# Experts of a two-block network in rounds of 1024 inner features, on one Trainium2 core

## The chip, the core and the metric

The program runs on one core of one Trainium2 chip. The core has five engines with a queue each, which run side by side and wait for each other by semaphores: TensorE (PE; its weight loads are shown apart as PEld), VectorE (DVE), ScalarE (ACT), GpSimd (POOL) and SyncE (SP), which here issues nearly all DMAs. Matrix products land in PSUM, which has eight banks of 128 partitions x 512 float32. The metric is the device time of one execution in microseconds (us). The kernel before takes 2576.64 us, the median of three runs (2575.73 to 2576.72).

## What is computed

Two blocks of a network run one after the other on 256 tokens of 1024 features, all in float32. The first block has two layers of attention; the second of them is followed by a mixture of experts, and this is the part that the change touches:

```python
def swiglu(h, wg, wu, wd):
    return (jax.nn.silu(h @ wg) * (h @ wu)) @ wd

def moe_swiglu(h, router, wg, wu, wd):
    logits = (h @ router).astype(jnp.float32)
    top_vals, top_idx = lax.top_k(logits, TOP_K)          # 2 of 8 experts for each token
    gates = jax.nn.softmax(top_vals, axis=-1)
    gate_e = jnp.sum(jax.nn.one_hot(top_idx, N_EXPERTS) * gates[..., None], axis=-2)
    ...
    for e in range(N_EXPERTS):
        out = out + gate_e[..., e:e + 1] * swiglu(h, wg[e], wu[e], wd[e])
    return out
```

`wg[e]` and `wu[e]` are 1024 x 3584, `wd[e]` is 3584 x 1024: 44.04 MB for one expert, 352 MB for eight. The second block (a gated feed-forward on tokens and on 256 context tokens, a mixer of a long convolution and attention, a second feed-forward) needs, among other things, the context's feed-forward, which depends on nothing of the first block; its pieces are strewn into the first block's stages as filling work.

## The kernel before

**Products.** A float32 operand is split into two parts, `hi` (rounded) and `lo` (the rest), whose sum is exact; `split` (L128 to L131) does it with a copy on ACT (L130) and a subtraction on DVE (L131). `mm3` (L133 to L137) makes one product of three: hi x hi (L135), hi x lo (L136), lo x hi (L137), each a matmul with 512 columns into one PSUM bank. So a weight must pass DMA, then ACT, then DVE, before L136 can use it.

**Weights.** They come in parts of 1 MB: a tile `raw` of 128 partitions x 2048 numbers, four buffers, loaded by one DMA on SP's queue (`wload`, L85). `wsplit` (L90) splits a part in two halves of 1024 numbers each into the tiles `whi` and `wlo`, three buffers each. `cuts` (L117) says what a part holds: for n columns of the matrix, 2048/n blocks of 128 rows. With n = 512 a part is four row blocks, and each row piece in memory is 512 numbers (2 KB); with n = 1024 it is two row blocks with pieces of 4 KB. Each part feeds 12 matmuls where 128 tokens are worked on, 24 where it is 256.

**The experts** (`moe`, L768 to L847). An expert takes at most 128 tokens. `gather` collects them by products with a 0/1 matrix (`xgh`, `xgl`: 32 small matmuls through the banks `mm`). Then, for f0 = 0, 512, ... 3072 (seven rounds), `ffn_gate` multiplies by 512 columns of `wg` (two parts, 24 matmuls, one PSUM bank `lin0`), ACT takes the silu of it (L313), `ffn_turn` transposes the round before's products (`hd` to `hh`, `hl`), `ffn_up` multiplies by 512 columns of `wu` (two parts, 24 matmuls), DVE multiplies silu and up (`hd`, L325), and `ffn_down` multiplies the round before's `hh`, `hl` by four row blocks of `wd` (two parts, 24 matmuls) into the two banks `acc`, which collect over all seven rounds. At the end of an expert `result` splits the sums into the tiles `yh`, `yl`, and `scatter` brings them back to their tokens (eight matmuls through banks `mm`), during the second round of the next expert. `hook("chunk")` puts in a piece of the context's work at every third round.

**PSUM.** Three banks `mm`, four `acc`, one `tp` (L71 to L82), the same for the whole program.

**Order.** The framework under the kernel plays the program through with costs of its own and writes the order of each engine's queue from that: a matmul that would have to wait can be put behind a later one, and splits stand ahead of what uses them as far as their buffers and the expected arrival of the data let them. On the chip each queue then runs strictly in that order. So where ACT's queue has a silu that waits for PE, the splits behind it wait, too; the same holds for `hd` on DVE.

## Time and profile before

The profile is of one execution, 2576.6 us from its first to its last instruction, which is also its device time to within 0.1 us. The stage of the experts is the stretch from about 703 to 1785 us.

| | share of the span |
|---|---|
| PE busy | 97% (2511.3 us, 12201 matmuls) |
| PEld busy | 78% |
| DVE busy | 71% (77 to 88% in the experts' stage) |
| ACT busy | 57% (70 to 76% in the experts' stage) |
| DMA | 71% of 16 engines (87 to 99% in the experts' stage) |

How to read it: a matmul with 512 columns is shown with 0.39 us from its start to its end, but the next one starts 0.23 us after it, so that PE's busy time covers up small waits; they show in the distance between starts, and in the weight loads (PEld), which stand idle in front of a matmul whose weights or data are late. The DMA share is that of the 16 DMA engines' time spent on packets.

### The profile page before, as it was taken

To read this page: it belongs to the slowest core of one execution; us is meant where nothing else is said; L and a number is where in the kernel's file an instruction comes from. 1 tells how busy PE (TensorE), PEld (TensorE's weight loads), DVE (VectorE), ACT (ScalarE), POOL (GpSimd) and SP (SyncE) were. 2 spreads that over 40 slices of the span, in tenths; PEclk is the share of its full clock that TensorE was granted. 3 is DMA by queue.
4 is the path that set the end of the run, shared out by engine and by line. 5 is a ranking of instruction groups with operands and counts; after the bars stand their busy time and mean duration, and the time that the engine had idled before them with its cause. 6 is when DMAs were issued, how large, how long until landed. Compare 5 with 4: busy or idle time off the path is not lost.

```text
span 2576.6 us, 31558 instructions
## 1 busy us (share of the span) xinstructions
PE 2511.3 (97%) x12201; PEld 2014.7 (78%) x12201; DVE 1818.5 (71%) x2272; ACT 1471.9 (57%) x1963; POOL 107.1 (4%) x128
## 2 busy tenths in 40 slices
PE   8999999999899999999999999999999999899998
PEld 5777777777788888888778787887778888777887
DVE  4655544656678888888888888888655667866444
ACT  3554333455477777777777777777443556434433
POOL 1000000110000000000000000000000110200000
PEclk9999999999999999999999999999999999999999
DMA  7746777544489999999999999997755553355552
GB/s 275 246 153 238 272 246 261 167 154 157 127 309 324 334 338 329 345 339 344 339 343 360 342 364 351 353 341 271 250 180 183 205 169 95 107 189 180 187 180 82
DMA packets 302175, 646.05 MB, mean 251 GB/s; under 512 B 16275, under 2 KB 43716, under 8 KB 301636
## 3 DMA queue, kind: packets, MB, share of 16 engines
q1 hardware_dynamic: 296164, 638.74, 71.3%
q10 hardware_dynamic: 5856, 5.24, 0.6%
q8 instruction: 97, 1.59, 0.2%
q14 instruction: 58, 0.48, 0.1%
HBM read 637.56 MB, written 6.38 MB: 250 GB/s over the span
## 4 chain that ended last, share of the span: by engine, by line
PE 62%; DVE 5%; ACT 2%; DMA 2%; issue 1%; POOL 1%; POOLq 0%; DVEq 0%; ACTq 0%
PE lin L136 13%; PE lin L137 13%; PE lin L135 13%; PE acc L136 5%; PE acc L135 5%; PE acc L137 5%; DVE wlo L131 2%; PE tp L180 2%; ACT whi L130 1%; PE gather L785 1%; DMA raw<-in_moe_w_up 1%; DMA raw<-in_moe_w_gate 1%; DVE dmx L1353 1%; PE z L136 0%; PE z L135 0%
## 5 line engine op out<-in xcount | busy, mean ns | idle before, releaser
L131 DVE TENSOR_TENSOR wlo<-raw,whi 128x1024 fp32r<-128x1024 f32 x1108 | 1312.2, 1226 | 414.8 <-ACT whi L130 411.9
L130 ACT ACTIVATE whi<-raw 128x1024 fp32r<-128x1024 f32 x1108 | 1115.7, 1055 | 613.2 <-PE lin L137 271.2
L135 PE MATMUL lin<-whi,hTh 128*128 128x512 f32 (+1 forms) x1152 | 449.1, 391 | 3.3 <-ACT hTh L130 2.8
L136 PE MATMUL lin<-wlo,hTh 128*128 128x512 f32 (+1 forms) x1152 | 444.8, 387 | 0.5 <-DVE wlo L131 0.5
L137 PE MATMUL lin<-whi,hTl 128*128 128x512 f32 (+1 forms) x1152 | 444.7, 386 | 0.6 <-DVE hTl L131 0.6
L136 PE MATMUL lin<-wlo,xgh 128*128 128x512 f32 x896 | 356.0, 397 | 4.8 <-DVE wlo L131 4.4
L135 PE MATMUL lin<-whi,xgh 128*128 128x512 f32 x896 | 354.3, 395 | 0.0
L137 PE MATMUL lin<-whi,xgl 128*128 128x512 f32 x896 | 350.7, 391 | 0.0
L136 PE MATMUL acc<-wlo,hh 128*128 128x512 f32 x736 | 290.3, 394 | 0.8 <-DVE wlo L131 0.7
L137 PE MATMUL acc<-whi,hl 128*128 128x512 f32 x736 | 288.4, 392 | 0.4 <-DVE hl L131 0.4
L135 PE MATMUL acc<-whi,hh 128*128 128x512 f32 x736 | 282.8, 396 | 2.3 <-ACT hh L130 2.3
L135 PEld LDWEIGHTS lin<-whi,hTh 128*128 128x128 f32 x1152 | 218.5, 190 | 52.7 <-ACT hTh L130 3.8
L136 PEld LDWEIGHTS lin<-wlo,hTh 128*128 128x128 f32 x1152 | 218.5, 190 | 47.1 <-DVE wlo L131 4.0
L137 PEld LDWEIGHTS lin<-whi,hTl 128*128 128x128 f32 x1152 | 218.1, 189 | 47.4 <-DVE hTl L131 1.7
L136 PEld LDWEIGHTS lin<-wlo,xgh 128*128 128x128 f32 x896 | 168.8, 188 | 51.3 <-DVE wlo L131 17.6
L135 PEld LDWEIGHTS lin<-whi,xgh 128*128 128x128 f32 x896 | 168.8, 188 | 35.9 <-issue 0.4
L137 PEld LDWEIGHTS lin<-whi,xgl 128*128 128x128 f32 x896 | 168.8, 188 | 33.8
L135 PEld LDWEIGHTS acc<-whi,hh 128*128 128x128 f32 x736 | 138.1, 188 | 35.1 <-ACT hh L130 3.4
L136 PEld LDWEIGHTS acc<-wlo,hh 128*128 128x128 f32 x736 | 138.3, 188 | 32.7 <-DVE wlo L131 2.8
L137 PEld LDWEIGHTS acc<-whi,hl 128*128 128x128 f32 x736 | 138.1, 188 | 30.5 <-DVE hl L131 0.8
L313 ACT ACTIVATE sg<-lin 128x512 f32<-128x512 f32 (+1 forms) x94 | 54.9, 584 | 116.4 <-PE lin L137 116.3
L131 DVE TENSOR_TENSOR hl<-tp,hh 128x512 fp32r<-128x512 f32 (+1 forms) x106 | 71.4, 674 | 68.5 <-ACT hh L130 68.0
(390 smaller groups left out, 2438.8 us busy)
## 6 DMA issues: line engine op xcount, KB each, us to landing
raw<-in_moe_w_gate SPq DMA_DIRECT2D x112, 1024.0 KB, 6.5
raw<-in_moe_w_up SPq DMA_DIRECT2D x112, 1024.0 KB, 6.6
raw<-in_moe_w_down SPq DMA_DIRECT2D x112, 1024.0 KB, 6.7
raw<-in_w_ff_in SPq DMA_DIRECT2D x66, 1024.0 KB, 5.4
raw<-in_w_in SPq DMA_DIRECT2D x58, 1024.0 KB, 5.4
raw<-in_w_ada SPq DMA_DIRECT2D x36, 1024.0 KB, 7.0
raw<-in_w_ff_out SPq DMA_DIRECT2D x33, 1024.0 KB, 5.0
raw<-in_dense_w_gate SPq DMA_DIRECT2D x14, 1024.0 KB, 8.1
```

Source lines behind the costliest of these rows:

```text
L130: self.nc.scalar.activation(hi, src, AF.Copy)
L131: self.nc.vector.tensor_tensor(lo, src, hi.bitcast(F32), op=ALU.subtract)
L135: t.matmul(out, ah, bh, start=first, stop=False)
L136: t.matmul(out, ah, bl, start=False, stop=False)
L137: t.matmul(out, al, bh, start=False, stop=last)
L180: nc.tensor.transpose(tp[:, b * P:(b + 1) * P], src[:, (b0 + b) * P:(b0 + b + 1) * P], self.ident)
L313: self.nc.scalar.activation(s, p, AF.Silu)
L785: nc.tensor.matmul(p[:, b * CAP:(b + 1) * CAP], src[:, t, k * P:(k + 1) * P], Dm[:, t, e], start=t == 0, stop=t == NT - 1)
L1353: nc.vector.tensor_reduce(mx[:, m:m + 1], ps, axis=AX.X, op=ALU.max)
```

## The change

Experts work in rounds of 1024 inner features: f0 = 0, 1024, 2048 with 1024 columns and f0 = 3072 with 512, four rounds in place of seven. The gate and up weights of a wide round come as parts of two row blocks x 1024 columns (row pieces of 4 KB), four parts each; the last round has parts as before. Each part feeds two PSUM banks, `lin0` (the first 512 columns) and `lin1`. The transposes of the round before come in two batches, after gate and in the middle of up. The `down` step of a wide round has four parts. `result` no longer has tiles of its own: it takes the tiles `hh`, `hl` (one buffer each). In the experts' stage PSUM is shared out as five banks `mm`, two `xacc`, one `tp`; what asks for `acc` there gets an `mm`. Scatter moves to the middle of the second round's gate. The filling pieces of the context come at every 1.7th round instead of every third. (In the changed file the comments are gone, and line numbers are 10 to 50 higher.)

```diff
+    def banks(self, **n):
+        self.psst.close()
+        self.nbank = n
+        self.ps = self.psst.enter_context(self.tc.tile_pool(name="ps", bufs=1, space=PSUM, reuse_waits="tile"))
+
+    def bank(self, tag, name):
+        tag = tag if tag in self.nbank else "mm"
+        return self.ps.tile([P, 512], F32, tag=tag, bufs=self.nbank[tag], name=name)
...
-            first = [(ap, m, 512) for f0 in (0, 512) for w in (wg, wu) for _, m, ap in self.cuts(w[0], 0, KT, f0, 512)]
+            first = [(ap, m, 1024) for w in (wg, wu) for _, m, ap in self.cuts(w[0], 0, KT, 0, 1024)]
             self.run_ahead(first[:7], 2)
             self.overflow(hk, og, cnt_i)
+            self.banks(mm=5, xacc=2, tp=1)
...
                 def result(job):
-                    yh = pool.tile([P, D], F32R, tag="yh", bufs=1, name="yh")
-                    yl = pool.tile([P, D], F32R, tag="yl", bufs=1, name="yl")
+                    yh, yl = (v.rearrange("p b s -> p (b s)") for v in self.expert_h(pool))
...
+                rounds = [(f0, min(1024, F1 - f0)) for f0 in range(0, F1, 1024)]
...
-                    for f0 in range(0, F1, 512):
-                        job = dict(f0=f0, n=512, nt=1, hT=xg, e=e)
-                        self.ffn_gate(pool, job, wg[e])
+                    for f0, n in rounds:
+                        job = dict(f0=f0, n=n, hT=xg, e=e)
+                        pg = self.expert_lin(xg, wg[e], f0, n, lambda: e and f0 == 1024 and scatter(e - 1, y))
+                        s = [self.ffn_silu(pool, p) for p in pg]
                         if prev:
-                            self.ffn_turn(pool, prev)
-                        self.ffn_up(pool, job, wu[e])
-                        if f0 + 512 == F1 and e + 1 < NE:
-                            nxt = gather(e + 1)
+                            self.expert_turn(pool, prev, 0)
+                        pu = self.expert_lin(xg, wu[e], f0, n, lambda: prev and self.expert_turn(pool, prev, 1))
+                        job["hd"] = [self.ffn_gated(pool, *v) for v in zip(s, pu)]
+                        if f0 + n == F1 and e + 1 < NE:
+                            xg = gather(e + 1)
                         if prev:
                             if prev["f0"] == 0:
-                                acc = [[self.acc(f"acc0{h}") for h in range(2)]]
+                                acc = [self.bank("xacc", f"acc0{h}") for h in range(2)]
...
-                            self.ffn_down(prev, wd[prev["e"]], F1)
+                            self.expert_down(prev, wd[prev["e"]])
...
+    def expert_lin(self, xT, w, c0, n, half=None):
+        out = [self.mm(f"lin{h}")[:, :min(512, n - 512 * h)] for h in range(-(-n // 512))]
+        for k0, m, (wh, wl) in self.parts(w, 0, KT, c0, n):
+            if half and k0 == KT // 2:
+                half()
+            for h, o in enumerate(out):
+                hs = slice(h * 512, h * 512 + o.shape[1])
+                for k in range(k0, k0 + m):
+                    self.mm3(o, xT[0][:, k], xT[1][:, k], wh[:, k - k0, hs], wl[:, k - k0, hs], k == 0, k == KT - 1)
+        return out
+
+    def expert_h(self, pool):
+        return [pool.tile([P, 8, CAP], F32R, tag=v, bufs=1, name=v) for v in ("hh", "hl")]
...
-                  "chunk": every(3, lambda: both(1), 2),
+                  "chunk": every(1.7, lambda: both(1), 1),
                   "last": lambda: both(40)})
+        self.banks(mm=3, acc=4, tp=1)
```

How this moves instructions shows best at the end of `up`, where DVE's `hd` (silu times up) stands between splits of weights. This is DVE's queue before, in the sixth expert's second round; `wlo_11197` and `wlo_11205` are the parts of `up`, `wlo_11239` is the first part of `down`, and "x2" is both halves of a part:

```order
L131 TENSOR_TENSOR wlo_11197<-raw_11194,whi_11196 128x1024 x2
L131 TENSOR_TENSOR wlo_11205<-raw_11202,whi_11204 128x1024 x2
L131 TENSOR_TENSOR wlo_11239<-raw_11236,whi_11238 128x1024
L325 SCALAR_TENSOR_TENSOR hd_11234<-sg_11182,lin0_11193 128x512
L131 TENSOR_TENSOR wlo_11239<-raw_11236,whi_11238 128x1024
L131 TENSOR_TENSOR wlo_11247<-raw_11244,whi_11246 128x1024 x2
```

And now, in the fifth expert's third round; `wlo_11372` is the last part of `up`, `wlo_11396` the first of `down`:

```order
L142 TENSOR_TENSOR wlo_11345<-raw_11342,whi_11344 128x1024 x2
L142 TENSOR_TENSOR wlo_11372<-raw_11369,whi_11371 128x1024 x2
L336 SCALAR_TENSOR_TENSOR hd_11389<-sg_11287,lin0_11300 128x512
L336 SCALAR_TENSOR_TENSOR hd_11391<-sg_11289,lin1_11301 128x512
L142 TENSOR_TENSOR wlo_11396<-raw_11393,whi_11395 128x1024 x2
L142 TENSOR_TENSOR wlo_11416<-raw_11413,whi_11415 128x1024 x2
```

Before, a half of the first `down` part is split ahead of `hd`; now two `hd` stand ahead of both halves. PE's queue at the same place before; `whi_11238` and `wlo_11239` are the first `down` part, and `tp` is the transpose of this round's `hd`:

```order
L137 MATMUL lin0_11193<-whi_11204,xgl_10586 128x512
L135 MATMUL acc00_10933<-whi_11238,hh_11184 128x512
L135 MATMUL acc01_10934<-whi_11238,hh_11184 128x512
L136 MATMUL acc00_10933<-wlo_11239,hh_11184 128x512
L137 MATMUL acc00_10933<-whi_11238,hl_11185 128x512
L136 MATMUL acc01_10934<-wlo_11239,hh_11184 128x512
L137 MATMUL acc01_10934<-whi_11238,hl_11185 128x512
L135 MATMUL acc00_10933<-whi_11238,hh_11184 128x512
L135 MATMUL acc01_10934<-whi_11238,hh_11184 128x512
L180 MATMUL tp_11321<-ident_69,hd_11234 128x128 x4
L136 MATMUL acc00_10933<-wlo_11239,hh_11184 128x512
```

And now, from the last products of `up` on:

```order
L146 MATMUL lin1_11301<-whi_11371,xgh_10525 128x512
L147 MATMUL lin0_11300<-wlo_11372,xgh_10525 128x512
L148 MATMUL lin0_11300<-whi_11371,xgl_10526 128x512
L147 MATMUL lin1_11301<-wlo_11372,xgh_10525 128x512
L148 MATMUL lin1_11301<-whi_11371,xgl_10526 128x512
L146 MATMUL acc00_11108<-whi_11395,hh_11291 128x512
L146 MATMUL acc01_11109<-whi_11395,hh_11291 128x512
L191 MATMUL tp_11533<-ident_69,hd_11389 128x128 x4
L147 MATMUL acc00_11108<-wlo_11396,hh_11291 128x512
```

Before, eight products and the transposes stood between the end of `up` and the first product with the second half of `wlo`; now the first product with `wlo` comes after two products and the transposes. At the end of the last expert, where nothing but `result` stands between the last product and `scatter`, PE's queue was, before (`yh`, `yl` are result's tiles):

```order
L806 MATMUL scatter_14943<-yh_14937,DT_5424 128x512
L806 MATMUL scatter_14947<-yh_14937,DT_5424 128x512
L806 MATMUL scatter_14951<-yh_14937,DT_5424 128x512
L807 MATMUL scatter_14943<-yl_14938,DT_5424 128x512
L807 MATMUL scatter_14951<-yl_14938,DT_5424 128x512
L807 MATMUL scatter_14947<-yl_14938,DT_5424 128x512
L806 MATMUL scatter_14955<-yh_14937,DT_5424 128x512
```

And now, with five banks `mm`:

```order
L817 MATMUL scatter_14899<-hh_14893,DT_5424 128x512
L817 MATMUL scatter_14903<-hh_14893,DT_5424 128x512
L817 MATMUL scatter_14907<-hh_14893,DT_5424 128x512
L817 MATMUL scatter_14911<-hh_14893,DT_5424 128x512
L818 MATMUL scatter_14899<-hl_14894,DT_5424 128x512
```

The fourth product into a bank of its own no longer comes last.

## Rows read from the trace of the kernel before

**Rows 1.** The page's head.
```profile
span 2576.6 us, 31558 instructions
```

**Rows 2.** Windows of the stage: us, busy time of each engine (instructions), clock, DMA share, GB/s.
```profile
974.00:1110.00 136.00, 136.00 (x655) 113.54 (x654) 119.68 (x118) 97.56 (x109) 0.00 (x0) 1.00 0.96 340
1371.00:1498.00 127.00, 125.68 (x580) 102.27 (x579) 111.88 (x109) 94.84 (x109) 0.00 (x0) 1.00 0.99 352
1498.00:1629.00 131.00, 131.00 (x606) 107.10 (x606) 115.36 (x112) 98.85 (x113) 0.00 (x0) 1.00 0.98 355
```

**Rows 3.** Timeline of PE: start, us, instruction; experts 5 to 8 begin, last scatter.
```profile
1240.45 0.34 PE L785 MATMUL gather<-Dm,h_hi 128*128 128x128 f32 x2
...
1370.45 0.45 PE L785 MATMUL gather<-Dm,h_hi 128*128 128x128 f32 x3
...
1497.75 0.45 PE L785 MATMUL gather<-Dm,h_hi 128*128 128x128 f32 x3
...
1623.44 0.45 PE L785 MATMUL gather<-Dm,h_hi 128*128 128x128 f32 x3
...
1784.35 0.40 PE L807 MATMUL scatter<-yl,DT 128*128 128x512 f32 x1
```

**Rows 4.** Timeline of PE in a stretch without waits, `lin` of the third expert.
```profile
989.65 0.39 PE L135 MATMUL lin<-whi,xgh 128*128 128x512 f32 x1
...
994.42 0.39 PE L135 MATMUL acc<-whi,hh 128*128 128x512 f32 x1
```

**Rows 5.** The chain of waits, merged: start, us, what.
```profile
945.48 0.44 PE tp L180 x4
...
974.20 3.52 PE gather L785 x32
```

**Rows 6.** Waits from 1243 to 1785 us: total us, times, longest.
```profile
ACT whi L130 <- DMA raw<-in_moe_w_gate: 17.9, 20, 2.5
ACT whi L130 <- DMA raw<-in_moe_w_down: 15.5, 19, 3.3
PEld lin L136 <- DVE wlo L131: 14.8, 28, 1.2
...
PEld acc L136 <- DVE wlo L131: 2.8, 5, 1.0
```

**Rows 7.** DMA queue from 1393 to 1402 us: packets, MB, share of 16 engines.
```profile
q1 hardware_dynamic: 1647, 3.28, 100.6%
```

**Rows 8.** The same from 1387 to 1391 us, and from 1460 to 1465.
```profile
q1 hardware_dynamic: 401, 1.55, 97.7%
...
q1 hardware_dynamic: 501, 1.86, 102.9%
```

**Rows 9.** Timeline of DVE around an `hd`, fifth expert.
```profile
1319.76 3.50 DVE L131 TENSOR_TENSOR wlo<-raw,whi 128x1024 fp32r<-128x1024 f32 x3 [1.07 <-ACT whi L130]
1323.88 0.69 DVE L325 SCALAR_TENSOR_TENSOR hd<-sg,lin 128x512 f32<-128x512 f32 x1 [0.63 <-PE lin L137]
1324.49 5.76 DVE L131 TENSOR_TENSOR wlo<-raw,whi 128x1024 fp32r<-128x1024 f32 x5
```

**Rows 10.** Timeline of PE at the same place.
```profile
1323.46 0.39 PE L137 MATMUL lin<-whi,xgl 128*128 128x512 f32 x1
...
1325.51 0.60 PE L180 MATMUL tp<-ident,hd 128*128 128x128 f32 x4
1325.86 0.48 PE L136 MATMUL acc<-wlo,hh 128*128 128x512 f32 x1
```

**Rows 11.** Timeline of ACT: `result` of the last expert.
```profile
1780.20 0.60 ACT L130 ACTIVATE yh<-acc 128x512 fp32r<-128x512 f32 x1
1781.56 0.60 ACT L130 ACTIVATE yh<-acc 128x512 fp32r<-128x512 f32 x1 [0.76 <-PE acc L137]
```

**Rows 12.** Timeline of PE: the last product and a late scatter.
```profile
1781.13 0.39 PE L137 MATMUL acc<-whi,hl 128*128 128x512 f32 x1
...
1784.01 0.51 PE L806 MATMUL scatter<-yh,DT 128*128 128x512 f32 x1 [0.37 <-DVE x L808]
```

More of the change, by code (lines that the diff above doesn't have):

```diff
@@ L77, in tp @@
         if wide and self.turn:
[L78 to L79 removed]
+            return self.bank("acc", "tpa")
+        return self.bank("tp", "tp")
     def acc(self, name="acc"):
[L82 removed]
+        return self.bank("acc", name)
     def wload(self, ap, kt, n):
@@ L791, in result @@
                 def result(job):
-                    yh = pool.tile([P, D], F32R, tag="yh", bufs=1, name="yh")
-                    yl = pool.tile([P, D], F32R, tag="yl", bufs=1, name="yl")
+                    yh, yl = (v.rearrange("p b s -> p (b s)") for v in self.expert_h(pool))
                     for h in range(2):
                         hs = slice(h * 512, (h + 1) * 512)
-                        self.split(yh[:CAP, hs], yl[:CAP, hs], job["acc"][0][h][:CAP])
+                        self.split(yh[:CAP, hs], yl[:CAP, hs], job["acc"][h][:CAP])
                     return yh, yl
@@ L832, in moe @@
                                     nc.scalar.activation(DT[:CAP, e0:e0 + 2].rearrange("p e s -> p (e s)"), tp[:CAP], AF.Copy)
-                            self.ffn_down(prev, wd[prev["e"]], F1)
+                            self.expert_down(prev, wd[prev["e"]])
                             if f0 == 0:
                                 y = result(prev)
-                        if f0 == 512 and e > 0:
-                            scatter(e - 1, y)
                         if not self.ahead:
@@ L840, in moe @@
                         prev = job
-                    xg = nxt
                 hook("last")
@@ L844, in moe, with expert_turn, expert_down @@
                 prev["acc"] = acc
-                self.ffn_turn(pool, prev)
-                self.ffn_down(prev, wd[NE - 1], F1)
+                for i in range(2):
+                    self.expert_turn(pool, prev, i)
+                self.expert_down(prev, wd[NE - 1])
                 scatter(NE - 1, result(prev))
+    def expert_lin(self, xT, w, c0, n, half=None):
[10 more added lines that the diff above has]
+        return [pool.tile([P, 8, CAP], F32R, tag=v, bufs=1, name=v) for v in ("hh", "hl")]
+    def expert_turn(self, pool, job, i):
+        if i == 0:
+            job["h"] = self.expert_h(pool)
+        if 512 * i < job["n"]:
+            bs = slice(4 * i, 4 * i + job["hd"][i].shape[1] // P)
+            self.transposes(job["hd"][i], bs.stop - bs.start, hl=[v[:, bs] for v in job["h"]])
+    def expert_down(self, job, wd):
+        hh, hl = job["h"]
+        b0, nb = job["f0"] // P, job["n"] // P
+        for k0, m, (wh, wl) in self.parts(wd, b0, nb, 0, D):
+            order = [(k, h) for k in range(m) for h in range(2)]
+            if k0 + m == F1 // P:
+                order.sort(key=lambda v: v[1])
+            for k, h in order:
+                hs = slice(h * 512, (h + 1) * 512)
+                self.mm3(job["acc"][h], hh[:, k0 + k - b0], hl[:, k0 + k - b0], wh[:, k, hs], wl[:, k, hs],
+                         k0 + k == 0, k0 + k == F1 // P - 1)
     def overflow(self, hk, og, cnt_i):
@@ L1564, in run @@
         self.moe({"norm": lambda: ctx(1), "logits": lambda: ctx(1), "pos": lambda: ctx(1), "cnt": lambda: ctx(1),
-                  "chunk": every(3, lambda: both(1), 2),
+                  "chunk": every(1.7, lambda: both(1), 1),
                   "last": lambda: both(40)})
+        self.banks(mm=3, acc=4, tp=1)
         self.dbg("x_f1", self.x)
```

12 lines of the change are left out of this document (4 added, 8 removed).

## The prediction

> **What bounds the kernel now.** I read the windows of the stage first, to see which engine is full. In the sixth and seventh expert (the last two windows) PE is busy all the time or nearly, at the full granted clock (1.00, which is 2.4 GHz), and the DMA engines are at a share of 0.98 to 0.99 with 352 to 355 GB/s; DVE has 12% to spare, ACT a quarter [rows 2]. So two things are full at once, and the question is which of them gives way to the other. A busy PE hides small waits, so I then read starts in PE's timeline: where nothing waits, 21 products take 994.42 - 989.65 = 4.77 us, 0.227 us each [rows 4]. A batch of four transposes costs 0.44 us, a gather 3.5 us [rows 5]. From the program's order an expert has 336 products for gate and up, 168 for down and 8 for scatter: 512 x 0.227 = 116.3, seven batches 3.1, gather 3.5, together 122.9 us. The starts of the gathers [rows 3] give what it took: 130.0 us for the fifth expert, 127.3 for the sixth, 125.7 for the seventh. The sixth and seventh have two more batches each from the context, 123.8 us of work. The eighth, up to its last scatter, took 160.9 us, with 639 products and ten batches, 153.0 us of work. So PE lost 7.1 + 3.5 + 1.9 + 7.9 = 20.4 us in these four, and that is what there is to win here. The first four experts have the context's products between them, which use each weight twice; in the third the DMA share is 0.96 and PE busy throughout [rows 2]. I count nothing to be won there.
>
> The list of waits says what PE lost it to: its weight loads stood 14.8 us for the `wlo` of gate and up and 2.8 us for that of down, and behind that ACT waited 17.9 us for gate weights and 15.5 us for down weights [rows 6]. So in the second half of the stage the data come late, by a little.
>
> The profiled execution's span is 2576.6 us [rows 1], the median of the timed runs 2576.64; I add the sum to the former and need no correction.
>
> **The change part by part.** What it does not touch: the number of products, of transposes, of splits on ACT and DVE, of bytes and of 1 MB DMAs on SP's queue, and the counts of filling pieces (18 calls in either case, in like places). None of these gets a price.
>
> *Wide rows.* In three rounds of four the gate and up weights come in pieces of 4 KB in place of 2 KB. The trace has both kinds. A stretch with gate and up alone moved 3.28 MB in 9 us at a share of 1.006, which is 362 GB/s for full engines [rows 7]. Two stretches with down, whose rows are 4 KB today, give 397 and 362 GB/s [rows 8]. So the wide pieces are worth between nothing and 9.5%; I take the mean, 4.7%. It acts on 6/7 of two thirds of the bytes, 57%: 2.7% of the transfer time, which is about 125 us for an expert (127 us at 0.98). That is 3.4 us for an expert, but no more than it lost: 3.4 + 3.4 + 1.9 + 3.4 = 12.1 us, and as buffers are few some half microsecond stays in each: -10 us. The bounds are 0 (the lower end of the rate) and -17.6 (all that the weight loads stood for).
>
> The Trainium skill, "Perfetto Trace Analysis", section "DMA Optimizations", says that making transfers of 2 KB into 4 KB can improve the throughput dramatically where it binds. These rows show a few per cent at most; by the rule the term would be its far bound, -17.6, and the sum some 7 us lower.
>
> *DVE's queue at the end of up.* This is the term against. Before, DVE has at least one half of the first down part split when it comes to `hd`. In the changed queue this cover is gone in the last four experts: going through their twelve wide rounds, I count four in which both `hd` stand ahead of any `wlo` of down, and four in which one half stands between the two `hd`. In the first four experts one part or more stands ahead nearly everywhere. What it costs follows from a place today where the cover is just enough: `hd` starts 0.42 us after the start of the last product of up (1323.46 to 1323.88), DVE goes on 0.61 us later (1324.49), a half of `wlo` takes 5.76 / 5 = 1.15 us [rows 9], and PE takes it up some 0.1 us after that: at 1325.86 [rows 10], without losing anything, because eight products and the transposes stood between. Put the end of up at 0. In the new order `lin0` is complete two products before, its `hd` runs from about -0.25 to 0.35, the second to 0.95, a half of `wlo` ends at 2.1 and PE can go on at 2.2; it has two products and four transposes to do, 0.9 us. So it loses 1.3 us in each of the four rounds of the first kind. In the other kind the first half ends at 1.5, PE goes on at 1.6 and has lost 0.7; it then has six products, 1.36 us, and the second half, behind the second `hd`, can be used at 3.35: another 0.4. Sum: 4 x 1.3 + 4 x 1.1 = 9.6 us. The bounds are 0, where DVE's queue is behind anyway because data are late (the wait is then the same one), and 8 x 2.0 = 16, where no transposes fill. I take 9.6, as DVE stood idle 0.63 us before `hd` even with the half ahead of it [rows 9].
>
> *Result without tiles of its own.* `yh` could be written while PE was in its last six products; the copy of the first half began 1.4 us before that of the second [rows 11]. `hh` has one buffer, so now both copies come after the last product that reads it, 1781.13 + 0.43 at the end [rows 12]. The second copy is then late by half a microsecond, and ACT's and DVE's later splits with it. Eight ends of experts, half of them with one part ahead: +2 us, with bounds of 0 and 8 x 0.5 = 4. Against that, scatter has five banks: the wait for an earlier result's addition goes (0.37 us, [rows 12]), and the four products with `hh` can come first: -0.5 us at the end of the last expert, where nothing else covers it. In the other experts scatter lies between gate's parts, hidden either way.
>
> *Silu and transposes.* Two silus after 48 products cost ACT what two after 24 each did; before the second, ACT has one part of up ready in most rounds, as before. The second batch of transposes in the middle of up is the same 0.44 us. The new banks let `lin1`'s products go ahead while `wlo` is late, which makes gate and up more patient by two products. I price this at 0 and give it ±3.
>
> *The switch of banks.* It comes once on each side of the stage. On the near side PE stands for the branch around the overflow code anyway; on the far side the norm's transposes get banks that the last filling products may still hold. 0, within ±2.
>
> Sum: -10 + 9.6 + 2 - 0.5 = +1.1 us: 2576.6 + 1.1 = 2577.7 us.
>
> **The rivals.**
>
> *The data win (faster).* DVE's queue costs nothing because the same waits are there already, only elsewhere: late data hold PE at gate, DVE's pause lets the buffers fill, and what counts is the transfer time alone. For it: ACT waits for DMA nearly twice as long as PE is held (33.4 against 17.6 us, [rows 6]), and the DMA share is at its top. Against it: PE and not DMA was the fuller one in the seventh expert, which lost just 1.9 us. Then -10 is left with result's +2 and -0.5 and a part of DVE's price, 1: -7.5, 2569 us; at the far bound of the rate, 2561.
>
> *DVE's queue decides (slower).* Its place is the pair of `hd` at the end of up; its price the full 1.3 to 2.0 us in eight rounds, and some in the first four experts, 14 us; result costs 3. It decides from the point at which the wide rows bring less than 12 us. With the lower rate they bring 5: +12, 2589 us. For it: the cover was 0.5 part in most of these rounds, and rows 10 show that this was just enough. Against it: a pause of PE lets DMA run ahead, so part of the price is given back.
>
> *Wide rows bring nothing.* The limit is not in the packets but in the memory behind them: then the two stretches of 362 GB/s [rows 7, 8] are the rule and 397 the exception. Late data stay, DVE's pauses fall partly into them: 0 + 6 + 1.5, 2584 us.
>
> The Trainium skill, "DMA: Bandwidth & Descriptors", section "Where 436 GB/s comes from", speaks for this last one: it puts the limit of transfers out of HBM at about 358 GB/s for a core, which the 352 to 355 GB/s of the windows would have reached. The 397 GB/s of rows 8 speak against it.
>
> **How the numbers follow.** My forecast, no change to within its parts, 0.40; the data win 0.30; DVE's queue decides 0.18; wide rows bring nothing 0.12. A measurement of this kernel can tell some 0.2% from no change, 5.2 us: below 2571.4 is faster, above 2581.8 slower. The first rival is faster, the two others are slower, the forecast's own spread (2572 to 2582) is the same: faster 0.30, same 0.40, slower 0.30. The likeliest time is 2577.7. The range runs from 2564 to 2590: on either side it takes in a rival's time and leaves out its far end. The forecast's own range is 2572 to 2582.
>
> **What would show it.** Right: the four last experts together within 3 us of today's 543.9 us (1240.45 to 1784.35); PE's waits for the `wlo` of gate and up down by half, new ones for that of down, of about a microsecond, each behind a pair of `hd`; the DMA share there lower by 0.02 to 0.03. Wrong towards faster: no `wlo` waits at down longer than 0.5 us, and experts of 124 us. Wrong towards slower: these waits in the first four experts, too, or a DMA share of 0.98 still. The forecast also fails if the stage is as forecast and the norm after it starts later, which would be the banks or `result`.

## The result, and the profile after

The changed kernel takes 2589.47 us (median of 4 runs, 2587.57 to 2593.02), the kernel before 2576.18 us in its 4: ratio 1.0056, 95% interval 1.0044 to 1.0068. It is slower by some 13 us. The forecast of no change, 2577.7 us, was wrong; the time lies just inside the upper edge of its range, 2590 us.

The profiled execution of the changed kernel is the slowest of its four; it is 14.6 us longer than the one of before:

```profile
span 2591.2 us, 31548 instructions
```

Where the 14.6 us are, from the starts of gathers and of the last scatter. PE's timeline after has for the first, the fifth to the eighth gather and the last scatters (each row starts with us from the span's start):

```profile
704.20 1.09 PE L797 MATMUL gather<-Dm,h_hi 128*128 128x128 f32 x4 [7.41 <-PEq L903]
...
1246.45 1.45 PE L797 MATMUL gather<-Dm,h_hi 128*128 128x128 f32 x12
...
1373.25 0.33 PE L797 MATMUL gather<-Dm,h_hi 128*128 128x128 f32 x2
...
1501.54 0.33 PE L797 MATMUL gather<-Dm,h_hi 128*128 128x128 f32 x2
...
1628.95 0.33 PE L797 MATMUL gather<-Dm,h_hi 128*128 128x128 f32 x2
...
1793.68 1.10 PE L818 MATMUL scatter<-hl,DT 128*128 128x512 f32 x4
```

| us | before | after | difference |
|---|---|---|---|
| start to first gather | 703.4 | 704.2 | +0.8 |
| experts 1 to 4 | 537.1 | 542.3 | +5.2 |
| experts 5 to 8, to the start of the last scatter matmul (1784.35 [rows 3]; 1794.37 after) | 543.9 | 547.9 | +4.0 |
| from there to the end | 792.3 | 796.8 | +4.6 |

PE has as many products in these stretches as before (4311 of 512 columns in the eight experts, split between the halves to within one). So not even a third of the loss lies in the last four experts, where the forecast had its two large terms. The waits of experts 5 to 8 (1249 to 1795 us; total us, times, longest), beside [rows 6]:

```profile
ACT whi L141 <- DMA raw<-in_moe_w_gate: 24.1, 18, 3.9
...
ACT whi L141 <- DMA raw<-in_moe_w_down: 17.5, 22, 2.0
...
PEld lin L147 <- DVE wlo L142: 11.9, 25, 1.0
...
PEld acc L147 <- DVE wlo L142: 9.1, 10, 1.3
```

For gate and up the weight loads wait 2.9 us less than before, for down 6.3 us more. The transfer itself did what the forecast said. The windows of experts 6 and 7 (busy time of each engine, clock, DMA share, GB/s):

```profile
1373.00:1501.00 128.00, 126.28 (x580) 102.27 (x579) 111.96 (x110) 94.22 (x109) 0.00 (x0) 1.00 0.95 348
1501.00:1629.00 128.00, 126.85 (x585) 103.13 (x584) 112.39 (x109) 95.16 (x110) 0.00 (x0) 1.00 0.96 350
```

The share fell by 0.02 to 0.04 against [rows 2]; 348/0.95 is 366 GB/s for full engines where 352/0.99 was 356, 350/0.96 is 365 where 355/0.98 was 362: a rate higher by some 3% and under 1%. But ACT waits longer for the data of gate and of down than before.

Three kinds of places show the loss. *First, the end of up* (the place of [rows 9, 10], in the fifth expert; DVE's timeline, then PE's):

```profile
1285.95 1.28 DVE L336 SCALAR_TENSOR_TENSOR hd<-sg,lin 128x512 f32<-128x512 f32 x2
1287.15 3.49 DVE L142 TENSOR_TENSOR wlo<-raw,whi 128x1024 fp32r<-128x1024 f32 x3
```
```profile
1285.51 0.61 PE L146 MATMUL acc<-whi,hh 128*128 128x512 f32 x2
1286.69 0.66 PE L191 MATMUL tp<-ident,hd 128*128 128x128 f32 x4 [0.56 <-DVE hd L336]
1288.43 0.50 PE L147 MATMUL acc<-wlo,hh 128*128 128x512 f32 x1 [1.08 <-DVE wlo L142]
```

Both `hd` stand ahead of the first half of down, and PE stands 1.08 us for it (1.24 us by the distance of starts, which is used below). This is the forecast's mechanism at its forecast price of 1.3 us; four places of the last four experts have it.

*Second, a filling piece in the third expert.* DVE, PE, and the granted clock (the column behind POOL's busy time) there:

```profile
1091.25 1.29 DVE L1160 TENSOR_TENSOR ctx_y<-cacc,ctx_y 128x512 f32<-128x512 f32 x2 [1.71 <-PE cacc L148]
1092.45 1.22 DVE L142 TENSOR_TENSOR wlo<-raw,whi 128x1024 fp32r<-128x1024 f32 x1
1093.59 1.28 DVE L1160 TENSOR_TENSOR ctx_y<-cacc,ctx_y 128x512 f32<-128x512 f32 x2
1094.79 5.76 DVE L142 TENSOR_TENSOR wlo<-raw,whi 128x1024 fp32r<-128x1024 f32 x5
```
```profile
1094.21 0.48 PE L146 MATMUL lin<-whi,xgh 128*128 128x512 f32 x1
1097.19 0.69 PE L147 MATMUL lin<-wlo,xgh 128*128 128x512 f32 x1 [2.51 <-DVE wlo L142]
1097.68 0.63 PE L148 MATMUL lin<-whi,xgl 128*128 128x512 f32 x1
```
```profile
1093.00:1097.20 4.20, 1.69 (x11) 1.15 (x9) 4.20 (x6) 2.49 (x3) 0.00 (x0) 1.00 0.32 119
1097.20:1100.60 3.40, 3.40 (x8) 2.69 (x9) 3.40 (x4) 0.00 (x0) 0.00 (x0) 0.52 0.94 326
```

DVE's queue has the additions for the context, which wait for PE's last products of the piece, ahead of the splits that PE needs next. PE stands 2.5 us (2.8 us by the distance of starts); then its granted clock is 0.52, the level of 1.2 GHz, and eight products start 0.43 us apart instead of 0.23: 1.6 us more. These 4.4 us are most of what experts 1 to 4 lost; the kernel before has no wait of over 0.5 us there.

*Third, the norm behind the stage.* PE's timeline, before and after:

```profile
1794.02 1.09 PE L287 MATMUL tpa<-ident,xg 128*128 128x128 f32 x8 [1.37 <-DVE xg L277]
```
```profile
1801.90 0.49 PE L147 MATMUL lin<-wlo,hTh 128*128 128x512 f32 x1 [1.29 <-DVE wlo L142]
1804.94 1.97 PE L298 MATMUL tpa<-ident,xg 128*128 128x128 f32 x8 [2.54 <-DVE xg L288]
...
1807.56 0.63 PE L147 MATMUL lin<-wlo,hTh 128*128 128x512 f32 x1
1807.99 0.63 PE L148 MATMUL lin<-whi,hTl 128*128 128x512 f32 x1
```

From the last scatter matmul to the norm's first transposes 26 filling products stand in PE's order; before it was 32 (the expectations below count one more each). With fewer of them PE stands 2.54 us before the transposes (1.37 before), and the lower clock follows again (starts 0.43 us apart at the end of the rows). By PE's starts, 4.2 of the 4.6 us behind the stage are lost by the end of this norm.

### The profile page after: what moved, and what is told of

The parts are those of the page before. It is cut to its first block, busy times and chain, and to the rows that moved or that the text cites. A ratio compares the mean times of both kernels' runs of the same rounds, so it can differ in the third digit from the quotient of the medians.

```text
span 2591.2 us, 31548 instructions
## 1 busy us (share of the span) xinstructions
PE 2518.2 (97%) x12201; PEld 2017.5 (78%) x12201; DVE 1818.4 (70%) x2272; ACT 1471.4 (57%) x1963; POOL 109.0 (4%) x128
## 4 chain that ended last, share of the span: by engine, by line
PE 64%; DVE 4%; ACT 2%; issue 1%; DMA 1%; POOL 1%; ACTq 0%; POOLq 0%; DVEq 0%
PE lin L147 13%; PE lin L148 13%; PE lin L146 13%; PE acc L147 5%; PE acc L148 5%; PE acc L146 5%; DVE wlo L142 2%; PE tp L191 2%; PE gather L797 1%; ACT whi L141 1%; DMA raw<-in_moe_w_gate 1%; DVE dmx L1399 1%; PE z L147 1%; PE z L146 0%; PE z L148 0%
## 5 line engine op out<-in xcount | busy, mean ns | idle before, releaser
L146 PE MATMUL lin<-whi,xgh 128*128 128x512 f32 x896 | 343.7, 396 | 0.0
L141 ACT ACTIVATE hh<-tp 128x512 fp32r<-128x512 f32 (+1 forms) x106 | 61.9, 584 | 95.6 <-PE tp L191 83.1
```

Source lines behind the costliest of these rows:

```text
L141: self.nc.scalar.activation(hi, src, AF.Copy)
L146: t.matmul(out, ah, bh, start=first, stop=False)
```

## The experiments

Ratios are to the kernel before, with 95% intervals; "stage" is first gather to last scatter and "behind" from there to the end, both of the profiled execution; "clock" is the mean over the timed runs. A profile is a single execution: the fastest of its kernel's in h21, e5_chunk0 and gcov, the slowest in the changed kernel, nbcov, nbcovg0 and pool4. So differences of a microsecond or two in these columns say little.

| run | edit | median us (runs) | ratio, interval | stage | behind | clock |
|---|---|---|---|---|---|---|
| before | | 2575.84 (27) | | 1081.0 | 792.3 | 0.9926 |
| after | | 2589.47 (4) | 1.0056, 1.0044 to 1.0068 | 1090.2 | 796.8 | 0.9913 |
| e1_narrow | 2 KB pieces | 2593.25 (5) | 1.0064, 1.0050 to 1.0078 | 1092.4 | 795.5 | 0.9904 |
| e3_cover | down split ahead of `hd` | 2589.13 (5) | 1.0050, 1.0037 to 1.0064 | 1085.5 | 795.6 | 0.9914 |
| h21 | `hh` in halves | 2588.43 (5) | 1.0054, 1.0041 to 1.0068 | 1087.6 | 794.2 | 0.9914 |
| e5_chunk0 | pieces one round earlier | 2587.09 (5) | 1.0047, 1.0033 to 1.0061 | 1082.1 | 793.9 | 0.9908 |
| tail | switch before the scatter | 2589.57 (5) | 1.0053, 1.0040 to 1.0066 | 1090.0 | 792.3 | 0.9922 |
| b_banks | before, with the banks alone | 2578.88 (11) | 1.0013, 1.0004 to 1.0021 | 1079.3 | 795.6 | 0.9915 |
| c0cov | pieces and cover | 2582.89 (7) | 1.0030, 1.0019 to 1.0041 | 1081.1 | 796.7 | 0.9910 |
| pool4 | an eighth of splits on POOL | 2640.70 (5) | 1.0243, 1.0230 to 1.0257 | | | 0.9890 |
| nobank | without the banks | 2585.64 (5) | 1.0037, 1.0024 to 1.0051 | 1088.2 | 790.9 | 0.9922 |
| c0covnb | all three | 2590.09 (5) | 1.0053, 1.0039 to 1.0067 | 1089.4 | 792.5 | 0.9910 |
| b_chunk1 | before, pieces moved | 2580.99 (11) | 1.0019, 1.0010 to 1.0028 | 1083.0 | 794.9 | 0.9912 |
| gcov | gate split ahead of a piece | 2589.52 (5) | 1.0056, 1.0043 to 1.0069 | 1086.0 | 794.2 | 0.9912 |
| nbcov | without banks, cover | 2581.11 (11) | 1.0022, 1.0014 to 1.0031 | 1085.2 | 791.1 | 0.9927 |
| nbcovg | and gate split ahead | 2582.93 (11) | 1.0026, 1.0017 to 1.0035 | 1085.3 | 793.8 | 0.9923 |
| nbcovg0 | and pieces earlier | 2594.46 (6) | 1.0066, 1.0052 to 1.0081 | 1103.1 | 791.0 | 0.9908 |
| c0covt | pieces, cover, switch | 2580.74 (11) | 1.0014, 1.0005 to 1.0023 | 1082.6 | 791.1 | 0.9923 |
| c0covt_narrow | the same, 2 KB pieces | 2580.38 (11) | 1.0014, 1.0005 to 1.0023 | 1084.0 | 791.5 | 0.9927 |
| c0covt_h21 | the same, `hh` in halves | 2581.07 (11) | 1.0018, 1.0009 to 1.0027 | 1087.0 | 791.1 | 0.9920 |

**e1_narrow.**
```diff
+        step = 512 if narrow else n
+        for c in range(0, n, step):
+            self.nc.sync.dma_start(dst[:, :, c:c + step], ap[:, :, c:c + step])
```


> The changed kernel with its 1024-column gate and up parts fetched as two DMAs of 512 columns each, so in 2 KB pieces again; tiles, products, banks and order as in the changed kernel. Theory of the forecast (wide rows are worth 3.4 us for an expert where it is short of data): some 10 us slower than the changed kernel, 2597 to 2602 us, and PE's weight loads wait longer for the wlo of gate and up. Theory that the transfer gains nearly nothing by the pieces' length (those waits fell only from 7.5 to 5.3 us between the two kernels): 2588 to 2593 us, DMA share back up by 0.01 to 0.03 but PE's waits as they are.


3.8 us slower, but its interval overlaps that of the changed kernel, so it does not decide. In the trace the waits for gate and up are 11.9 us as with wide rows, the DMA share is back at 0.99 and 0.98. (c0covt_narrow says more, below. In both, a part is also two DMAs of 0.5 MB in place of one of 1 MB; no run separates this from the length of the pieces.)

**e3_cover.**
```diff
+                            k0, m, ap = next(self.cuts(wd[prev["e"]], prev["f0"] // P, prev["n"] // P, 0, D))
+                            early = k0, m, self.wsplit(ap, m, D)
                         job["hd"] = [self.ffn_gated(pool, *v) for v in zip(s, pu)]
...
-        for k0, m, (wh, wl) in self.parts(wd, b0, nb, 0, D):
+        rest = self.parts(wd, b0 + skip, nb - skip, 0, D)
+        for k0, m, (wh, wl) in chain([early] if early else [], rest):
```


> The changed kernel, but the first down part is split ahead of the two hd in the program, so that in DVE's queue both its halves stand ahead of them nearly everywhere. Theory that DVE's queue at the end of up is the loss: the waits for the wlo of down (7.4 us in the last four experts, 1.24 us at most places) go to under 2 us, 2583 to 2585 us. Rival, data late: the splits wait for their data and hold up the hd behind them instead; the sum of PE's waits in the last four experts stays within 2 us, 2588 to 2592 us.


By the distances of starts PE's waits for the `wlo` of down in the last four experts fell from 7.4 to 4.7 us, not under 2: three of the four places of 1.24 us went to 0.64. The time hardly moved (0.3 us); the stalls of the second and third kind were still there.

**h21.**
```diff
-        return [pool.tile([P, 8, CAP], F32R, tag=v, bufs=1, name=v) for v in ("hh", "hl")]
+        return [pool.tile([P, 4, CAP], F32R, tag=f"{v}{i}", bufs=(2, 1)[i], name=f"{v}{i}") for v in ("hh", "hl")]
```


> The changed kernel with hh and hl as two tiles of 512 each, the first with two buffers; result takes the same tiles. Theory that the one buffer of hh is what stops ACT (at 1085.7 us it stood 2.49 us before a copy into hh until the last product of down, and PE 2.8 us at 1094.2 and then 9 products at half the granted clock): this stall is gone, 4 to 5 us less before the fifth expert, and the copies of result no longer wait, 0.5 us for an end: 2583 to 2586 us. Rival: DVE would stand at the additions for the context, which wait for PE, all the same: under 1.5 us gained, 2588 to 2590 us.


The rival held, in time (1.0 us faster) and for the stall. ACT's copy no longer waits for the last product of down, but PE's row is still there:
```profile
1095.95 0.49 PE L147 MATMUL lin<-wlo,xgh 128*128 128x512 f32 x1 [2.49 <-DVE wlo L142]
1096.29 0.39 PE L148 MATMUL lin<-whi,xgl 128*128 128x512 f32 x1
1096.52 0.40 PE L146 MATMUL lin<-whi,xgh 128*128 128x512 f32 x1
```

**e5_chunk0** (`every(1.7, lambda: both(1), 0)` for `..., 1)`).


> The changed kernel with the filling pieces from the context called one round earlier (skip 0 in place of 1); nothing else. Theory that the 4.8 us at 1094 us and the 4.6 us after the stage are matters of where the pieces fall and not of the wide rows, banks or queues: either is gone or in another place, and the time moves by 3 to 8 us, 2580 to 2586 us if both are gone. Rival, they belong to the rounds themselves: 2588 to 2591 us, with like stalls.


The stall at 1094 us is gone and the stage is within 1.1 us of before in the profile, which is the fastest of the five runs. In the median it is 2.4 us faster than the changed kernel, with intervals that overlap. The timed runs spread from 2582.5 us at a mean clock of 0.993 to 2590.2 at 0.989: how much of the time has the lower clock differs from run to run.

**tail.**
```diff
-                scatter(NE - 1, result(prev))
+                last = result(prev)
+                self.banks(mm=3, acc=4, tp=1)
+                scatter(NE - 1, last)
...
-        self.banks(mm=3, acc=4, tp=1)
```


> The changed kernel with the second switch of PSUM banks put ahead of the last expert's scatter instead of behind the stage. In PE's order the norm's transposes then stand behind 33 products again, as in the kernel before, and not behind 27. Theory that the switch is what the norm after the stage pays for: the waits of 1.46 and 2.81 us there fall back to some 1.7 together, and the products at half clock behind them go: 3 to 4.5 us faster than the changed kernel, 2585 to 2586 us. Rival, the norm's chain (additions to x, means, xg) sets that time whatever stands around it: 2588 to 2591 us.


The work behind the stage is back at 792.3 us and the clock at 0.992, yet the median is that of the changed kernel, as the rival had it, though not for the rival's reason: in the trace the norm's wait is back at 1.64 us. What takes the gain away is not shown, but for 1.07 us that scatter with three banks now waits for the additions. Not decided by time; the place of the norm's waits is.

**b_banks** (the kernel before, with `banks(mm=5, xacc=2, tp=1)` over the stage).


> The kernel before with the changed kernel's sharing of PSUM banks alone (5 for mm, 2 for the accumulators, 1 for transposes, over the stage); rounds of 512, its tiles and pieces as they were. In PE's order the norm's transposes stand behind 27 products as in the changed kernel. Theory that the switch costs the norm: the two waits appear here, too, 3 to 4 us slower than before, 2578 to 2580 us; if the context's accumulators, now in mm's banks, also hold up the first experts, more. Rival, the forecast's term of 0 within 2: 2573 to 2577 us.


Some 3 us slower (1.0 to 5.4 by the ratio): the sharing of banks has a price of its own. In the profile its stage is even shorter, and 3.3 us more lie behind it:
```profile
1792.01 0.50 PE L146 MATMUL lin<-wlo,hTh 128*128 128x512 f32 x1 [1.16 <-DVE wlo L141]
1795.06 1.23 PE L297 MATMUL tpa<-ident,xg 128*128 128x128 f32 x8 [2.54 <-DVE xg L287]
```

**c0cov** (e3_cover and e5_chunk0 together).


> The changed kernel with both the pieces called one round earlier and the first down part split ahead of the two hd. Theory that the losses add up: no stall at 1094 us, waits for the wlo of down under 3 us, and with fewer waits of over a microsecond a granted clock back at 0.992: 2581 to 2584 us. Rival, each edit only moves the stalls: 2586 to 2590 us, with new ones of over a microsecond elsewhere in the first four experts.


The stage is that of the kernel before, 1081.1 us; what is left lies behind it. Cover is worth 4.2 us here by the medians (2587.09 to 2582.89; the runs overlap) and was worth 0.3 with the stall in place. The mean clock did not come back; the norm's long wait, which was left in, fits that.

**pool4** (one half in eight of the weights' splits, from the experts' stage on: 86 of them in the stage and 29 behind it, where the expectation has them in the stage alone).
```diff
-        self.nc.vector.tensor_tensor(lo, src, hi.bitcast(F32), op=ALU.subtract)
+        (self.nc.gpsimd if pool else self.nc.vector).tensor_tensor(lo, src, hi.bitcast(F32), op=ALU.subtract)
```


> The changed kernel with one in eight of the weight splits' subtractions in the experts' stage done on POOL in place of DVE. Theory that DVE is what PE waits for and not data: DVE's busy time in a window of an expert falls by a tenth, the wlo waits of the last four experts (12.7 us in PE's rows) by half, 2582 to 2585 us. Rival, data: the waits stay, 2588 to 2591 us. A third: a subtraction of 128 x 1024 takes POOL 2.4 to 3.8 us by the rows of before, PE reaches such a half before it is ready, and it is slower than the changed kernel, 2592 us and up.


The third theory, by far. It says nothing on DVE against data, since POOL's halves are late themselves; see the last section.

**nobank** (no `banks` calls; the experts' sums in two of four `acc`).


> The changed kernel without its own sharing of PSUM banks: 3 for mm, 4 for accumulators (the context's, too), 1 for transposes throughout, no switch on either side; rounds of 1024 as in the changed kernel, so the fourth product tile of a round waits for the first silu to free a bank. Theory that the sharing is one of the causes (alone it made the kernel before 3.4 us slower): 3 to 5 us faster than the changed kernel, 2584 to 2587 us, the waits after the stage as before it. Rival, the bank that the second up tile waits for costs as much in 32 rounds as the switch gave: 2588 to 2595 us, with waits at the start of up.


3.8 us faster than the changed kernel, as b_banks has it from the other side. PE has no wait over 0.3 us from 1085 to 1100 us here, so the stall in the third expert did not come without the sharing, in which the context's accumulators take `mm`'s banks: sharing and place of the pieces make it together (e5_chunk0 does without it, too). A new one (1.83 us at 1270.9) came in the fifth expert.

**c0covnb** (c0cov and nobank).


> All three together: no bank sharing of its own, the pieces one round earlier, the first down part split ahead of the two hd. Theory that these three are what the change lost and that rounds of 1024 with wide rows cost and bring nearly nothing by themselves: 2574 to 2579 us, the same as the kernel before. Rival, the losses come back elsewhere: 2582 to 2588 us.


The rival, and slower still: 2590 us. With the banks back the scheduler lays the moved pieces otherwise, and PE stands at 1234 and 1621 us (1.8 us each, and the lower clock after both).

**b_chunk1** (the kernel before, `every(3, ..., 1)` for `every(3, ..., 2)`).


> A control on the kernel before: its filling pieces called one round of 512 earlier (skip 1 in place of 2), nothing else. Theory that any such move costs as much as the change did: 2580 to 2590 us. Rival, the kernel before is not sensitive to it, since its rounds of 512 leave half a part of cover nearly everywhere: 2573 to 2579 us.


5 us slower (2.6 to 7.2 by the ratio), with nothing else changed. The row of its worst place:
```profile
1238.60 0.50 PE L135 MATMUL lin<-whi,xgh 128*128 128x512 f32 x1 [2.63 <-ACT whi L130]
```

**gcov, nbcov, nbcovg, nbcovg0.** nbcov is nobank with e3_cover; gcov, and the g in the others, is:
```diff
...
+                                raw = self.wload(ap, m, n2)
...
+                                    self.split(hi[:, j:j + 1024], lo[:, j:j + 1024], raw[:, j:j + 1024])
+                                held = hi, lo
                             hook("chunk")
+                            if ge < NE:
+                                self.ahead.append(held)
```


> The changed kernel with the first part of the next gate split ahead of each filling piece in the program. Theory that the stall of 2.76 us at 1094 us is DVE's queue, in which the context's additions stand ahead of gate's splits and wait for PE: it is gone, 3 to 5 us faster than the changed kernel, 2584 to 2587 us. Rival: the held part takes one of three buffers from the piece, whose own splits are then late; 2588 to 2593 us.

> The changed kernel without its bank sharing and with the first down part split ahead of the two hd; pieces where the change has them. Theory that cover and banks add up where no piece interferes: 2581 to 2584 us, waits for the wlo of down under 4 us in the last four experts. Rival, as in the run of all three: 2586 to 2590 us.

> The same, and the first part of the next gate split ahead of each piece, too. Theory that what is left is DVE's queue: 2576 to 2580 us, no wait over 1.3 us on PE between the second and the eighth expert. Rival, the place of the pieces: 2582 to 2588 us.

> The same with the pieces one round earlier. Queue theory: within 2 us of the run with the pieces where the change has them. Rival, the place of the pieces: 4 us or more apart from it, with a stall of over 2 us at the end of the fourth expert, as in the run of all three and in the control on the kernel before.


gcov takes the stall in the third expert down from 2.5 to 1.2 us; the time did not move. nbcov is the sum of banks (nobank, -3.8) and cover (as in c0cov, -4.2): 2581.5 expected from these, 2581.1 measured. More cover (nbcovg) adds nothing to it, and with the pieces a round earlier the same kernel is 11.5 us slower. So what nbcov still lacks is not DVE's cover; that the place of the pieces can cost as much is shown, that it is all of the rest is not. Most of the 11.5 us are one wait: nbcovg0 has a place at which DVE cannot overwrite a tile of the context whose transfer to memory is under way, and with it every split behind:
```profile
1469.98 0.41 DVE L304 TENSOR_SCALAR hf<-tpa,A,B 128x128 f32<-128x128 f32 x1 [8.77 <-DMA hcd<-hf]
```

**c0covt, c0covt_narrow, c0covt_h21** (c0cov with tail; with e1_narrow; with h21).


> The changed kernel with the pieces one round earlier, the first down part split ahead of the two hd, and the second switch of banks ahead of the last scatter. Theory that cover, place of the pieces and switch are the whole loss: the stage as in the run without the third (last scatter some 1081 us after the first gather, as in the kernel before), the work behind it 792 us as before: 2575 to 2579 us, no difference from the kernel before. Rival, rounds of 1024 cost something of their own: 2581 to 2585 us.

> The same with gate and up parts fetched as two DMAs of 512 columns, in 2 KB pieces. If wide rows are worth what the forecast said (10 us): 8 us or more slower than the same with wide rows. If PE's waits come from queues and not from data: within 3 us of it, though the DMA share in the last experts goes up by 0.02 or more.

> The same with hh and hl as two tiles of 512, the first with two buffers, which result uses, too. The forecast's +2 us for result without tiles of its own: 1 to 3 us faster than with one hh. Rival, no difference, within 1.5 us, since the copies' wait is hidden at all ends but the last.


In c0covt's profile the stage and the work behind are those of the kernel before to within 2 us (the stage is 3.0 us longer with narrow rows, 6.0 with `hh` in halves), but the median is still 4.9 us above it (3.6 by the ratio, 1.3 to 5.9), nearer to what the rival said. Wide rows bring nothing that eleven runs each can tell: 2580.74 and 2580.38 us, the same ratio with the same interval. That leaves room for 2 or 3 us, not for 10. Windows of the sixth and seventh expert, wide, then narrow:
```profile
1372.00:1498.00 126.00, 125.10 (x576) 101.75 (x577) 110.99 (x109) 93.36 (x108) 0.00 (x0) 1.00 0.95 349
1499.00:1627.00 128.00, 125.67 (x580) 102.64 (x580) 114.25 (x110) 96.21 (x110) 0.00 (x0) 1.00 0.99 358
```
```profile
1370.00:1497.00 127.00, 125.69 (x578) 102.19 (x578) 111.52 (x109) 93.71 (x108) 0.00 (x0) 1.00 1.00 352
1497.00:1626.00 129.00, 126.51 (x579) 103.59 (x578) 114.67 (x111) 96.15 (x109) 0.00 (x0) 0.99 0.99 354
```
For full engines that is 367 against 352 GB/s in the sixth expert, 4% more, and 362 against 358 in the seventh, 1% more. The halves of `hh` gain nothing either: 2581.07 us.

## Why the prediction was wrong

**The step that failed first: "wide rows ... 3.4 us for an expert ... -10 us".** The rate came out near the forecast's 2.7% (3% and under 1% in two windows of the changed kernel); its conversion into time did not. Measured between c0covt and c0covt_narrow: wide rows 0.4 us slower by the medians, which is nothing within the spread. With 0 in its place the forecast's own sum is 2587.7 us. That this comes near 2589.5 is partly luck: DVE's term was some 5 us too high, and the banks and the filling pieces, both at 0, were too low by somewhat more. The profile page's list of DMA issues shows no gain either (median us from issue to landing, last number), before and after:
```profile
raw<-in_moe_w_gate SPq DMA_DIRECT2D x112, 1024.0 KB, 6.5
raw<-in_moe_w_up SPq DMA_DIRECT2D x112, 1024.0 KB, 6.6
raw<-in_moe_w_down SPq DMA_DIRECT2D x112, 1024.0 KB, 6.7
```
```profile
raw<-in_moe_w_gate SPq DMA_DIRECT2D x112, 1024.0 KB, 6.1
raw<-in_moe_w_up SPq DMA_DIRECT2D x112, 1024.0 KB, 6.4
raw<-in_moe_w_down SPq DMA_DIRECT2D x112, 1024.0 KB, 7.0
```
The three add up to 19.8 and 19.5 us: a part lands hardly sooner after its issue. The forecast read a share of 0.98 and ACT's waits for DMA as a shortage of rate. That a part is asked for only when one of four buffers comes free, and that this sets the waits, fits the rows, but no run changed the number of buffers: argued, not shown.

The Trainium skill, "Perfetto Trace Analysis", section "DMA Optimizations", calls larger transfers, such as 4 KB for 2 KB, the primary optimisation where DMA binds. Here they lowered the share in some windows (0.95 against 1.00) and the time not at all (2580.74 against 2580.38 us).

**"DVE's queue at the end of up ... 9.6 us": right in kind, half in size.** The waits came where forecast, 6.3 us more of them in PE's weight loads [rows 6]. Covering the place gave 0.3, 4.2 and 4.5 us (e3_cover; c0cov; nbcov); only in the last pair do the runs of the two kernels hardly overlap. By PE's starts the first kind, both `hd` ahead, cost 1.24 us at four places, for 1.3 forecast. The second kind, one half between the two `hd`, was priced at 1.1 us at four places: one lost 1.2 us, another 0.7, the others a quarter each. Together that is 7.4 us for 9.6, and the kernel before had 1.3 us of such waits.

**"The switch of banks ... 0, within 2": mis-sized.** Some 3 and 3.8 us, from both sides (b_banks, nobank). The forecast saw that "the norm's transposes get banks that the last filling products may still hold", but took its price as the wait alone. The order in which they then stand, six filling products sooner, made a wait of 2.5 us, and the lower clock behind it: in every profile with 26 products ahead of the transposes the wait is 2.4 to 2.6 us, in every one with 32 it is 1.4 to 1.7. The mean clock goes with this: 0.9904 to 0.9915 in the runs with the changed order (pool4, with its own waits, 0.9890), 0.9920 to 0.9927 where it is put back (tail, nobank, nbcov, nbcovg, the three c0covt). The exceptions, c0covnb, nbcovg0 and b_chunk1 with 0.9908 to 0.9912, have new stalls of their own. For a PE that is always busy, 0.001 of 2580 us is 2.6 us; tail, which has the clock back and not the time, shows that this is not the whole sum.

**"the counts of filling pieces (18 calls in either case, in like places). None of these gets a price": failed.** The count is not the cost, the place is: one round's shift costs the untouched kernel 5 us, nbcov 9.0 (c0covnb) and nbcovg 11.5, and takes the worst stall out of the changed kernel (e5_chunk0). In the changed kernel the place made, with the banks, the stall in the third expert, in the half where the forecast said "I count nothing to be won there" and did not ask what could be lost.

**"Result without tiles of its own ... +2" and scatter's "-0.5": nothing measurable.** Tiles for result gained nothing (c0covt_h21, 0.3 us slower); that the other work of the experts' ends hides the copies' wait is argued, not shown. Five banks did let scatter's matmuls go at once, but what the norm's transposes then wait for is DVE's `xg` behind the additions to x.

**What was to show it:** the last four experts within 3 us of 543.9 (4.0 over), the waits for gate and up halved (14.8 to 11.9 only), new ones of a microsecond at down (they came), a share lower by 0.02 to 0.03 (0.04 and 0.02), and as a way to fail, "the norm after it starts later" (it did).

**The rival "DVE's queue decides", 2589 us,** has the time, and its cause is only a third of it: queue some 4 us, banks 3 to 4, the place of the pieces about as much (the 4.4 us in the third expert), wide rows nothing to be seen. "Wide rows bring nothing" was right in its name; its reason, a limit in the memory, was not, since the rate did rise. "The data win" fell with the first step.

**Open.** c0covt, with the three causes taken out, stays 3.6 us (1.3 to 5.9) above the kernel before. In its profile the first gather starts at 707.2 us, in that of before at 703.4, in those of the other versions at 702.8 to 707.3, though up to there the queues of PE, DVE and ACT hold the same instructions in the same order in all of them (PE's order first differs at 718 us). So in this profile 3.8 of the 4.3 us by which it is longer lie ahead of the first instruction of these queues that differs. Of these, 1.5 us come with the clock in the first 56 us. Windows of before, then of c0covt:

```profile
49.00:54.00 5.00, 5.00 (x22) 4.05 (x23) 3.28 (x3) 1.45 (x2) 0.00 (x0) 1.00 1.04 391
```
```profile
49.00:54.00 5.00, 4.46 (x13) 3.50 (x13) 4.00 (x4) 2.16 (x3) 0.00 (x0) 0.66 1.01 357
```

One execution cannot say whether the other ten runs lose their time there, too, so the cause of these 3.6 us stays open. No version tried beats the kernel before.

## What to carry to other kernels

A resource at 0.98 of its time is a bound only if work arrives sooner when it is relieved: look at the time from issue to landing and at what releases the next request before pricing a gain in rate. Where a scheduler writes in-order queues, an edit to banks or to the place of filling work reorders what stands far away: price it by a control that moves only that, on the kernel before. And a pause of PE of one to three microseconds can cost 1.6 us more than its length, in lower clock, and need not.

## What the runs showed of the hardware

*The price of a pause.* After PE stood 2.5 us in the third expert its granted clock was 0.52 for 3.4 us (1.6 us lost); behind the same pause in h21 (2.49 us, its rows above) the products start 0.23 us apart, at full level. Behind the wait of 1.08 us in the fifth expert the clock stayed at full level in the profile of the changed kernel, but fell behind the same wait in those of e1_narrow and h21. The same kernel differed by 7.6 us in five runs (e5_chunk0), the slower at the lower mean clock.

*POOL can hold DVE up.* In pool4 a subtraction of 128 x 1024 took POOL 2.63 us in the mean, DVE 1.23 before; and DVE's can stand while POOL's runs. POOL's row, then DVE's:
```profile
1299.26 2.93 POOL L146 TENSOR_TENSOR wlo<-raw,whi 128x1024 fp32r<-128x1024 f32 x1 [11.12 <-ACT whi L145]
```
```profile
1299.89 3.39 DVE L146 TENSOR_TENSOR wlo<-raw,whi 128x1024 fp32r<-128x1024 f32 x1
```
DVE's ends 1.1 us after POOL's, about its usual length. Not each overlap costs that: of DVE's subtractions that overlapped one of POOL's, more than half kept their usual length, and the mean was 1.60 us, against 1.23 of those that did not. The Trainium skill, "SBUF — State Buffer", section "Who interferes with whom", states it: a DVE instruction with two inputs in SBUF contends with a GpSimd one that reads SBUF. The trace agrees, by the 3.39 us of this row. With PE waiting for the slower halves on top, one split in eight on POOL cost 51 us over the changed kernel.
